# Split-ahead weight units: their loads wait for the activation or residual update that precedes them in the program

## The chip, the cores and the metric

The kernel runs on one core of one Trainium2 chip, as a single launch. The metric is the device time of that launch in microseconds (us), from the start of the program to its end. The times of the kernel before are three runs without a profiler, and one further execution that was profiled.

## The reference

A two-layer transformer over 512 tokens of width 1024, in float32. Each layer is a feed-forward block (FFN1), a mixer of several attention kinds, and a second feed-forward block (FFN2); every one adds to the residual stream x.

```python
def swiglu_ffn(x, g, w_gate, w_up, w_down):        # w_gate, w_up: 1024 x 2816; w_down: 2816 x 1024
    h = rmsnorm(x, g)
    return (jax.nn.silu(h @ w_gate) * (h @ w_up)) @ w_down

for i in range(DEPTH):                              # DEPTH = 2
    x = x + 0.5 * swiglu_ffn(x, ffn1_norm[i], ...)
    h = rmsnorm(x, mix_norm[i])
    if i % 2 == 0:
        x = x + even_mixer(h, cos, sin, ev_w_in[e], ..., ev_w_out[e])   # w_in 1024 x 2468, w_out 1024 x 1024
    else:
        x = x + odd_mixer(h, cos, sin, cos_i, sin_i, od_w_in[o], od_w_out[o])  # w_in 1024 x 2340
    x = x + 0.5 * swiglu_ffn(x, ffn2_norm[i], ...)
return rmsnorm(x, final_norm)
```

## The kernel before, in words

**Precision.** Every large product is made of three matmuls of a faster type. A float32 operand is split into a high part h (a rounded copy, by ScalarE, here ACT) and a low part l (the operand less h, by VectorE, here DVE). `mm3` then adds the products high-high, high-low and low-high. Activations are split once; weights are split as they arrive. `cut` (line 321) is the split of a weight tile: line 325 on ACT, line 326 on DVE.

**Weights of the feed-forward blocks.** `wunit` loads 128 x 1024 numbers into a buffer `raw` by SyncE's DMA queue (SP) and cuts them into `wh` and `wl`. There are four buffers of each.

**The feed-forward block.** `ffn` goes over eleven chunks of 256 hidden columns in three groups: chunks 0 to 3, 4 to 7 and 8 to 10. For each chunk `gate_up` makes the gate and up products and from them the activations `at`, split into two parts. From the second or third chunk on the up product is done by `seven`, a seven-product scheme (Strassen's kind): it loads two `raw` tiles (line 694), adds blocks of them on DVE (`s`, lines 720 to 723), splits the sums on ACT and DVE (lines 704 and 705), and combines the seven products (lines 737 to 751). A product on GpSimd (POOL) at line 777 multiplies the gate by the row scale `rb`. After each group `proj_T` does the down projection in four blocks of 256 output columns; each block ends with two residual updates `x[c] = ps * 0.5 + x[c]` on DVE (`update`, line 581). The gate and up products of a group read the normalised input of the block and not these updates.

**Split-ahead units.** The weights of the two mixers (60 units of at most 128 x 1024 numbers, 32 for the even layer and 28 for the odd one) are not cut in the mixers. The generator `cut_ahead` (line 267) does it earlier: it loads a unit into a buffer `craw` (two of them) by POOL's DMA queue, cuts it into `ch` and `cl` (two each), and stores both to scratch memory (`cuth`, `cutl`, line 282, also POOL's queue). The mixers later load the parts from there. One step of the generator cuts unit i, stores unit i-1 and issues the load of unit i+1.

**Where the program advances it.** `ffn` takes one step after the chunks 3, 5, 6 and 7, and weaves steps into the down projections: `per` units for each block of a down projection, and in the last group only in its first two blocks. The even-layer generator is advanced in FFN1 of layer 0 with `per` 3, the odd-layer one in FFN2 of layer 0 and then in FFN1 of layer 1 with `per` 2. What is left is run after the block.

**What sets the order.** The kernel is written on a layer that schedules at build time. It puts the instructions of each engine into a fixed queue, as its own model of time finds their operands and buffers ready, with the program's order as the priority, and adds the semaphores. An instruction may so be moved ahead of others that precede it in the program, if it doesn't depend on them. `pin` (keep in program order) prevents this, but only while `pinned[0]` is true, and that is set to false with the last slice of each block's first chunk. On the chip each engine runs its queue in order.

Of the kernel before, what the change touches and what calls it, by code (L numbers as in the profile page):

```python
# [13 lines left out]
F32 = mybir.dt.float32  # L14
# [51 lines left out]
def hybrid_kernel(tc, x_in, positions, ffn1_norm, ffn1_w_gate, ffn1_w_up, ffn1_w_down, mix_norm,  # L66
# [3 lines left out]
    nc = tc.nc  # L70
    with ExitStack() as ctx:
# [6 lines left out]
        def nm(p):  # L78
            cnt[0] += 1
            return f"{p}_{cnt[0]}"  # L80


        def ps_tile(tag):
            return psp.tile([P, S], F32, tag=tag, bufs=PSUM_BUFS[tag], name=nm("ps" + tag))

        def tile_(tag, dt=F32R):
            return sb.tile([P, S], dt, tag=tag, bufs=SB_BUFS[tag], name=nm(tag))
# [7 lines left out]
        def pin(ins):  # L95

            return tc.keep_in_program_order(ins) if pinned[0] else ins
# [29 lines left out]
        rows = cst.tile([16, P], F32, name="rows")  # L127
# [36 lines left out]
        x = [cst.tile([P, S], F32, name=f"x{c}") for c in range(NC)]  # L164
# [87 lines left out]


        cut_units = {}

        def wunit(src, a, b, rows=False, key=None, tag=("raw", "wh", "wl")):

            n = a * b  # L260
            if key in cut_units:
                res = []
                for part, t in zip(cut_units[key], tag[1:]):
                    w = sb.tile([P, 1024], F32R, tag=t, bufs=W_BUFS, name=nm(t))
                    nc.sync.dma_start(w[:, :n].bitcast(F32), part)
                    res.append(w[:, :n].rearrange("p (a b) -> p a b", a=a))
                return res
            h, l = cut(load_raw(src, a, b, rows, tag[0], RAW_BUFS), n, tag[1:], W_BUFS)
            return (h[:, :n].rearrange("p (a b) -> p a b", a=a), l[:, :n].rearrange("p (a b) -> p a b", a=a))

        def cut_ahead(units):

            raw = done = None

            def store():
                key, n, tiles = done
                parts = []
                for t, c in zip(tiles, "hl"):  # L280
                    d = scr.tile([P, n], F32, tag=nm("cut" + c), name=nm("cut" + c))
                    nc.gpsimd.dma_start(d, t[:, :n].bitcast(F32))
                    parts.append(d)
                cut_units[key] = parts

            for i, (key, src, a, b, rows) in enumerate(units):
                n = a * b
                if raw is None:
                    raw = load_raw(src, a, b, rows, "craw", 2, nc.gpsimd)
                now = key, n, cut(raw, n, ("ch", "cl"), 2)  # L290
                if done is not None:
                    store()
                done = now
                if i + 1 < len(units):
                    raw = load_raw(*units[i + 1][1:], "craw", 2, nc.gpsimd)
                yield
            store()

        def load_raw(src, a, b, rows, tag, bufs, queue=nc.sync):
            n = a * b  # L300
            raw = sb.tile([P, 1024], F32, tag=tag, bufs=bufs, name=nm(tag))
            r3 = raw[:, :n].rearrange("p (a b) -> p a b", a=a)
            if rows:
                o = 0
                for sap in src:
                    pin(queue.dma_start(r3[:, o:o + sap.shape[1]], sap))
                    o += sap.shape[1]
            elif isinstance(src, list):
                o = 0
                for sap, wd in src:  # L310
                    dst = r3[:, :, o:o + wd]
                    if len(sap.shape) == 4:
                        for c in range(a):
                            queue.dma_start(dst[:, c].rearrange("p (k d) -> p k d", k=sap.shape[2]), sap[:, c])
                    else:
                        queue.dma_start(dst, sap)
                    o += wd
            else:
                queue.dma_start(r3, src)
            return raw  # L320

        def cut(raw, n, tags, bufs):

            h, l = (sb.tile([P, 1024], F32R, tag=t, bufs=bufs, name=nm(t)) for t in tags)
            pin(nc.scalar.activation(h[:, :n], raw[:, :n], AF.Copy))  # L325
            pin(nc.vector.tensor_sub(l[:, :n], raw[:, :n], h[:, :n].bitcast(F32)))  # L326
            return h, l

        def mm3(ps, lh, ll, rh, rl, start, stop):
            nc.tensor.matmul(ps, lh, rh, start=start, stop=False)  # L330
            nc.tensor.matmul(ps, lh, rl, start=False, stop=False)  # L331
            nc.tensor.matmul(ps, ll, rh, start=False, stop=stop)  # L332
# [168 lines left out]
        def split(src, width=S, tag="f"):  # L501

            h, l = tile_(tag), tile_(tag)
            nc.scalar.copy(h[:, :width], src)
            nc.vector.tensor_sub(l[:, :width], src, h[:, :width].bitcast(F32))
            return h, l
# [70 lines left out]
        def update(c, ps, scale, nxt):  # L577
            if scale == 1.0:
                nc.vector.tensor_add(x[c], ps, x[c])
            else:  # L580
                nc.vector.scalar_tensor_tensor(x[c], ps, scale, x[c], op0=ALU.mult, op1=ALU.add)
            if nxt is not None:
                nxt.add(c)

# [168 lines left out]
        def gate_up(wg, wu, k, norm, sums, at):  # L753

            f0 = 256 * k
            if k < (1 if norm.source is None else 2):
                gate_up_pair(wg, wu, f0, norm, k == 0, sums.work, at)
                return
            psg = [ps_tile("T"), ps_tile("T")]
            for hf in range(2):  # L760
                h, l = wunit(wg[hf * 512:(hf + 1) * 512, f0:f0 + 256].rearrange("(c p) f -> p c f", p=P), 4, 256)
                if hf:
                    norm.rstd()
                for f in range(2):
                    if hf and f:
                        norm.finish()
                    for c in range(4):
                        xh, xl = norm.xg[hf * 4 + c]
                        mm3(psg[f], h[:, c, f * P:(f + 1) * P], l[:, c, f * P:(f + 1) * P], xh, xl,
                            hf == 0 and c == 0, hf == 1 and c == 3)  # L770
            rb = norm.rstd_row()
            gs, up = [], [tile_("p", F32) for _ in range(2)]
            for f in range(2):
                g = tile_("p", F32)
                nc.vector.tensor_mul(g, psg[f], rb)  # L775
                nc.scalar.activation(g, g, AF.Silu)  # L776
                nc.gpsimd.tensor_mul(g, g, rb)  # L777
                gs.append(g)
            seven(wu, f0, sums, up)
            nc.vector.tensor_mul(up[0], up[0], gs[0])  # L780
            at.append(split(up[0]))
            nc.vector.scalar_tensor_tensor(up[1], up[1], -1.0, gs[1], op0=ALU.mult, op1=ALU.mult)
            at.append(split(up[1]))

        def ffn(norm, wg, wu, wd, nxt, hook=None, ahead=iter(()), per=2, early=None):

            sums = Sums(norm)
            for p0, p1 in GROUPS:
                at = []
                for k in range(p0, p1):  # L790
                    gate_up(wg, wu, k, norm, sums, at)
                    if hook is not None and k < 6:
                        next(hook, None)
                    if k in (3, 5, 6, 7):
                        run(take(ahead, 1))
                for d0 in range(0, D, 256):
                    part = per / (4 * (p1 - p0)) if p1 < 11 or d0 < 512 else 0.0
                    run(weave(proj_T(wd[256 * p0:256 * p1], at, d0,
                                     lambda c, ps: update(c, ps, 0.5, nxt if p1 == 11 else None)), ahead, [part]))
                    if p1 == 11 and d0 == 0 and early is not None:  # L800
                        early()
# [741 lines left out]
        def hook():  # L1543
# [7 lines left out]
            tabs.extend(rope_tables(pos_f))  # L1551

        ev_ahead = cut_ahead(units_of(even_sources(), ev_w_out[0], "ev", EV_ORDERS))
        od_ahead = cut_ahead(units_of(odd_sources(), od_w_out[0], "od", OD_ORDERS))
        for layer in range(2):
            nm_ = Norm(1, layer)
# [46 lines left out]
```

## Time and profile before

| | us |
|---|---|
| median of 3 runs | 2079.99 |
| lowest and highest | 2079.59, 2083.52 |
| the profiled execution's own time | 2085.85 |
| its span, first to last instruction | 2084.1 |

Busy shares of the span: PE (TensorE matmuls) 95%, its weight loads 84%, DVE 67%, ACT 43%, POOL 21%. Mean DMA traffic 139 GB/s. The mean granted clock of TensorE is 0.978 of its full speed.

The profile has these views. The slices cut the span in 40 equal parts, 52.1 us each, and give busy tenths. The windows give sums for chosen stretches. The chain of waits follows the work that ended last back in time. The waits say who waited for whom. A tile's view says how often and when it was written or read.

### The profile page before, as it was taken

The numbers are of one execution on the slowest core, as the hardware profiler recorded it, in microseconds if no ns is written. First come the engines' busy times: TensorE is split into PE (matmuls) and PEld (weight loads), VectorE is DVE, ScalarE is ACT, GpSimd is POOL, SyncE is SP. The second block draws the span as 40 slices with busy tenths as digits, with TensorE's granted clock in tenths as the row PEclk, the third lists the DMA queues.
The fourth block names the chain that finished last, engine by engine and source line by source line (L and its number), as shares of the span: only waits on it lengthen the run. The fifth ranks groups of instructions, "written<-read, shape, count | busy, mean of one in ns | idle before, by whom it ended". The sixth has DMA issues, their size and how long they took to land.

```text
span 2084.1 us, 30295 instructions
## 1 busy us (share of the span) xinstructions
PE 1979.7 (95%) x11575; PEld 1751.5 (84%) x11575; DVE 1389.0 (67%) x2448; ACT 893.2 (43%) x1570; POOL 430.2 (21%) x584
## 2 busy tenths in 40 slices
PE   7897888899999999999999999999999999999998
PEld 5785776789997778889898888889998888889898
DVE  6775774754458768657477756747599778657464
ACT  6543442432456755324245323323326665324243
POOL 3544433301223411001010201101012211001012
PEclk9998899899999999999999999999999999999999
DMA  9797799673320123332323333323542223332321
GB/s 297 243 334 267 260 332 344 222 250 132 122 92 19 38 77 112 112 91 92 112 81 112 90 106 89 111 87 100 173 163 83 89 94 100 105 98 92 111 82 61
DMA packets 191811, 290.36 MB, mean 139 GB/s; under 512 B 12825, under 2 KB 154929, under 8 KB 191665
## 3 DMA queue, kind: packets, MB, share of 16 engines
q1 hardware_dynamic: 161152, 197.75, 29.6%
q0 software_dynamic: 23776, 84.30, 11.6%
q10 hardware_dynamic: 6736, 6.37, 0.9%
q8 instruction: 91, 1.49, 0.3%
q14 instruction: 56, 0.45, 0.1%
HBM read 230.11 MB, written 58.26 MB: 138 GB/s over the span
## 4 chain that ended last, share of the span: by engine, by line
PE 61%; issue 12%; DVE 12%; DMA 9%; POOL 3%; ACT 3%; DVEq 0%; POOLq 0%; ACTq 0%
PE psB L330 8%; PE psB L331 8%; PE psB L332 8%; PE psT L331 5%; PE psT L330 5%; PE psT L332 5%; PE psG L330 5%; PE psG L332 5%; PE psG L331 5%; DMA cutl<-cl 4%; DMA raw<-in_ffn_w_up_dram 2%; DMA craw<-in_ev_w_in_dram 2%; DVE cl L326 1%; ACT p L929 1%; DVE f L1428 1%
## 5 line engine op out<-in xcount | busy, mean ns | idle before, releaser
L326 DVE TENSOR_TENSOR wl<-raw,wh 128x1024 fp32r<-128x1024 f32 (+1 forms) x198 | 256.4, 1296 | 85.5 <-ACT wh L325 81.0
L777 POOL TENSOR_TENSOR p<-p,p 128x512 f32<-128x512 f32 x78 | 123.2, 1582 | 758.2 <-ACT p L776 730.4
L325 ACT ACTIVATE wh<-raw 128x1024 fp32r<-128x1024 f32 (+1 forms) x198 | 197.4, 1003 | 189.8 <-PE psB L331 162.1
L332 PE MATMUL psT<-xg,wl 128*128 128x512 f32 x704 | 275.6, 392 | 0.9 <-DVE wl L326 0.9
L330 PE MATMUL psT<-xg,wh 128*128 128x512 f32 x704 | 275.9, 392 | 0.0
L331 PE MATMUL psT<-xg,wh 128*128 128x512 f32 x704 | 275.1, 391 | 0.0
L330 PE MATMUL psB<-f,wh 128*128 128x512 f32 x656 | 255.5, 390 | 0.0
L331 PE MATMUL psB<-f,wh 128*128 128x512 f32 x656 | 255.3, 389 | 0.0
L332 PE MATMUL psB<-f,wl 128*128 128x512 f32 x656 | 255.2, 389 | 0.0
L330 PE MATMUL psG<-t7h,wh 128*128 128x256 f32 x624 | 185.1, 297 | 25.0 <-ACT k L737 22.1
L332 PE MATMUL psG<-t7h,wl 128*128 128x256 f32 x624 | 183.8, 294 | 6.7 <-DVE wl L705 6.7
L331 PE MATMUL psG<-t7l,wh 128*128 128x256 f32 x624 | 183.0, 293 | 0.0
L332 PEld LDWEIGHTS psT<-xg,wl 128*128 128x128 f32 x704 | 132.9, 189 | 29.3 <-DVE wl L326 1.3
L330 PEld LDWEIGHTS psT<-xg,wh 128*128 128x128 f32 x704 | 132.9, 189 | 26.7
L331 PEld LDWEIGHTS psT<-xg,wh 128*128 128x128 f32 x704 | 132.8, 189 | 26.5
L330 PEld LDWEIGHTS psG<-t7h,wh 128*128 128x128 f32 x624 | 127.1, 204 | 27.9 <-ACT k L737 23.6
L332 PE MATMUL psG<-xg,wl 128*128 128x256 f32 x468 | 135.1, 289 | 15.9 <-DVE wl L705 15.9
L330 PE MATMUL psB<-wh,xg 128*128 128x256 f32 x512 | 148.7, 290 | 0.4 <-DVE sa L927 0.4
L332 PE MATMUL psB<-wh,xg 128*128 128x256 f32 x512 | 145.3, 284 | 0.0
L331 PE MATMUL psB<-wl,xg 128*128 128x256 f32 x512 | 144.9, 283 | 0.0
L332 PEld LDWEIGHTS psB<-f,wl 128*128 128x128 f32 x656 | 123.1, 188 | 25.9
L776 ACT ACTIVATE p<-p 128x512 f32<-128x512 f32 x78 | 49.2, 631 | 222.1 <-DVE p L775 222.1
(312 smaller groups left out, 4802.2 us busy)
## 6 DMA issues: line engine op xcount, KB each, us to landing
raw<-in_ffn_w_down_dram SPq DMA_DIRECT2D x168, 256.0 KB, 3.3
raw<-in_ffn_w_gate_dram SPq DMA_DIRECT2D x80, 512.0 KB, 3.9
raw<-in_ffn_w_up_dram SPq DMA_DIRECT2D x80, 512.0 KB, 4.4
cuth<-ch POOLq DMA_DIRECT2D x44, 512.0 KB, 6.4
cutl<-cl POOLq DMA_DIRECT2D x44, 512.0 KB, 6.8
wl<-cutl SPq DMA_DIRECT2D x44, 512.0 KB, 3.7
wh<-cuth SPq DMA_DIRECT2D x44, 512.0 KB, 4.4
craw<-in_od_w_in_dram POOLq DMA_DIRECT2D x16, 512.0 KB, 6.6
```

The costliest lines, as they stand in the source:

```text
L325: pin(nc.scalar.activation(h[:, :n], raw[:, :n], AF.Copy))
L326: pin(nc.vector.tensor_sub(l[:, :n], raw[:, :n], h[:, :n].bitcast(F32)))
L330: nc.tensor.matmul(ps, lh, rh, start=start, stop=False)
L331: nc.tensor.matmul(ps, lh, rl, start=False, stop=False)
L332: nc.tensor.matmul(ps, ll, rh, start=False, stop=stop)
L776: nc.scalar.activation(g, g, AF.Silu)
L777: nc.gpsimd.tensor_mul(g, g, rb)
L929: nc.scalar.activation(pr[i], pr[i], AF.Exp, scale=-1.0, bias=ng[:, i:i + 1], accum_out=rs[:, i:i + 1])
L1428: nc.vector.match_replace(out=bd[i], in_to_replace=m8, in_values=bd[i], imm_value=-3e38)
```

## The change

The code gets a one-element list `mark`. `update` writes into it the first column of the residual tile it has just updated; `gate_up`, on its path with `seven`, the first column of the high part of the activation it has just split. With the new argument `gate=True`, which only `cut_ahead` passes, `load_raw` first copies that column on POOL into the first column of the new `craw` tile. The load overwrites it, and so comes after it. The value copied is never used.

```diff
+        mark = [None]
...
                 if raw is None:
-                    raw = load_raw(src, a, b, rows, "craw", 2, nc.gpsimd)
+                    raw = load_raw(src, a, b, rows, "craw", 2, nc.gpsimd, True)
...
                 if i + 1 < len(units):
-                    raw = load_raw(*units[i + 1][1:], "craw", 2, nc.gpsimd)
+                    raw = load_raw(*units[i + 1][1:], "craw", 2, nc.gpsimd, True)
...
-        def load_raw(src, a, b, rows, tag, bufs, queue=nc.sync):
+        def load_raw(src, a, b, rows, tag, bufs, queue=nc.sync, gate=False):
             n = a * b
             raw = sb.tile([P, 1024], F32, tag=tag, bufs=bufs, name=nm(tag))
+            if gate:
+
+                nc.gpsimd.tensor_copy(raw[:, 0:1], mark[0])
...
                 nc.vector.scalar_tensor_tensor(x[c], ps, scale, x[c], op0=ALU.mult, op1=ALU.add)
+            mark[0] = x[c][:, 0:1]
...
             at.append(split(up[1]))
+            mark[0] = at[-1][0][:, 0:1].bitcast(F32)
```

## Rows read from the trace of the kernel before

**Rows 1.** The page's 40 slices: busy tenths, granted clock, DMA share.
```profile
PE   7897888899999999999999999999999999999998
...
PEclk9998899899999999999999999999999999999999
DMA  9797799673320123332323333323542223332321
```

**Rows 2.** Chain of waits in order of time: start us, us, what.
```profile
15.90 0.80 PE psS L330
```

**Rows 3.** Windows of FFN1, layer 0: us, engines' busy us (instructions), clock, DMA share, GB/s.
```profile
0.00:124.00 124.00, 104.19 (x523) 87.63 (x524) 93.24 (x128) 73.12 (x99) 58.11 (x98) 0.97 0.87 283
124.00:181.00 57.00, 52.32 (x235) 42.92 (x234) 29.87 (x54) 15.69 (x18) 20.47 (x32) 1.00 0.91 302
181.00:300.00 119.00, 91.35 (x491) 82.11 (x492) 88.29 (x111) 51.53 (x71) 53.26 (x76) 0.83 0.82 279
300.00:348.00 48.00, 48.00 (x214) 39.74 (x213) 24.25 (x28) 15.75 (x16) 16.02 (x26) 1.00 0.97 346
348.00:431.00 83.00, 63.89 (x367) 58.01 (x366) 56.55 (x75) 31.75 (x43) 25.91 (x33) 0.86 0.62 227
431.00:461.00 30.00, 30.00 (x136) 24.79 (x135) 17.09 (x24) 11.21 (x18) 0.64 (x1) 1.00 0.91 302
```

**Rows 4.** Windows of FFN2, layer 0, the same six stages (PE, PEld, DVE, ACT, POOL).
```profile
777.00:865.00 88.00, 85.64 (x495) 75.56 (x494) 70.53 (x105) 43.79 (x62) 14.22 (x9) 0.98 0.34 102
865.00:908.00 43.00, 43.00 (x191) 35.62 (x190) 19.38 (x24) 8.52 (x9) 0.00 (x0) 1.00 0.37 110
908.00:995.00 87.00, 87.00 (x543) 78.88 (x543) 63.61 (x89) 35.23 (x49) 13.22 (x8) 1.00 0.30 92
995.00:1036.00 41.00, 41.00 (x183) 33.95 (x182) 17.15 (x21) 7.55 (x8) 0.00 (x0) 1.00 0.37 115
1036.00:1102.00 66.00, 66.00 (x411) 59.81 (x410) 47.37 (x67) 25.60 (x37) 9.58 (x6) 1.00 0.28 84
1102.00:1131.00 29.00, 29.00 (x129) 24.01 (x129) 17.72 (x26) 13.47 (x20) 0.00 (x0) 1.00 0.33 102
```

**Rows 5.** The tile craw: ns min/median/max, first and last start us.
```profile
L325 ACT ACTIVATE ch<-craw x60: 630/1057/1067, 13.9 to 395.1; 128x1024 fp32r<-128x1024 f32 x44, 128x512 fp32r<-128x512 f32 x8, 128x840 fp32r<-128x840 f32 x4, 128x584 fp32r<-128x584 f32 x4
...
L316 POOL DMA_DIRECT2D craw<-in_od_w_in_dram x20: 717/766/811, 225.4 to 331.9; - x20
...
DMA to landing us min/median/max: 3.0/6.1/9.1
```

**Rows 6.** Windows of FFN1, layer 0, of ACT's instructions on ch alone.
```profile
0.00:124.00 124.00, 15.28 (x15) 0.97 0.87 283
124.00:181.00 57.00, 8.05 (x8) 1.00 0.91 302
181.00:300.00 119.00, 18.80 (x22) 0.83 0.82 279
300.00:348.00 48.00, 8.50 (x8) 1.00 0.97 346
348.00:431.00 83.00, 7.37 (x7) 0.86 0.62 227
```

**Rows 7.** PE's waits, 777 to 1131 us: total, times, longest us; the longest.
```profile
PE psX L560 <- DVE p L546: 2.0, 1, 2.0
```

**Rows 8.** Waits of all engines, 0 to 461 us: total, times, longest us.
```profile
DVE cl L326 <- DMA cutl<-cl: 44.5, 13, 6.9
...
ACT ch L325 <- DMA craw<-in_od_w_in_dram: 36.4, 12, 6.6
...
PE psG L332 <- DVE wl L705: 22.6, 9, 6.7
```

**Rows 9.** POOL's groups by shape: busy us, mean ns; idle before.
```profile
L843 POOL TENSOR_TENSOR sm<-sm,keep 128x1 f32<-128x1 f32 x4 | 2.2, 546 | 0.3
...
L842 POOL TENSOR_SCALAR sm<-sm,sm 128x1 f32<-128x1 f32 x4 | 1.1, 265 | 6.1 <-ACT pt L832 6.1
```

## The prediction

> **What bounds the kernel now.** I read the page's slices first [rows 1]: TensorE (PE) is 90% busy or more almost everywhere after the first fifth of the span, while in the first eight slices (0 to 417 us) it stands at 70 to 90%, its granted clock dips to 80 and 90%, and the 16 DMA engines are 60 to 90% busy, against mostly 10 to 40% after the first quarter. So the one stretch with slack is the first feed-forward block (FFN1 of layer 0, 0 to 461 us); the others run at PE's pace.
>
> How much slack: I cut this block into its six stages (gate/up of chunks 0 to 3, down of group 0, gate/up 4 to 7, down, gate/up 8 to 10, down) and set each beside the same stage of FFN2 of layer 0 (777 to 1131 us), which does the same matmuls with the ordinary traffic [rows 3, 4]. PE works across stage borders, so I count matmuls: the excess of a stage is its length less its matmuls at the later block's pace.
> - A, 0 to 124: 124 - 523 x 88/495 = 31 us, of which 16 are the start: the chain of waits reaches the first weight matmul at 15.90 us [rows 2].
> - B, 124 to 181: 57 - 235 x 43/191 = 4.
> - C, 181 to 300: 119 - 491 x 87/543 = 40.
> - D, 300 to 348: 48 - 214 x 41/183 = 0.
> - E, 348 to 431: 83 - 367 x 66/411 = 24.
> - F, 431 to 461: 30 - 136 x 29/129 = -1.
>
> Without the start that is 15 + 4 + 40 + 0 + 24 - 1 = 82 us, the most that a change confined to this block's side work can give back. In C and E the granted clock is 0.83 and 0.86, that is, part of the time at 1.2 instead of 2.4 GHz; in the later block's same stages it is 1.00, and one PE wait of 2.0 us is the longest there [rows 4, 7].
>
> What makes the excess: the split-ahead units. All 60 are cut between 13.9 and 395.1 us, and the loads from od_w_in, whose generator is first advanced in FFN2, start at 225.4 us [rows 5]. The order in each engine's queue is made at build time; nothing that these loads read depends on the program's progress, so they went as far forward as buffers allowed. Counted by stage [rows 6]: 15, 8, 22, 8, 7 and none. Per unit that is 1.0 us in A, 0.5 in B, 1.83 in C, 0.0 in D, 3.4 in E. The way it costs is in the waits [rows 8]: ACT stands at `ch` for a landing load, DVE stands at `cl` until an earlier store of `cutl` has landed, the weight splits queued behind them come late, and PE waits for `wl`. Down stages hide it (weights are split several units ahead), the seven-product stages don't.
>
> **The change part by part.**
> *60 copies of one column on POOL.* The trace before has no such copy; the nearest rows are POOL instructions on 128x1, 265 and 546 ns [rows 9]. At most 60 x 0.55 = 33 us on an engine that is 21% busy; at the low end nothing is seen of it. A gain is excluded, as it only adds work. I take nothing, since it precedes a load of 6.1 us median landing [rows 5] that is not on PE's path by itself. Loads and stores keep their number and their bytes.
>
> *What the copy waits for.* For the 28 odd-layer units this moves the work: the first load cannot start before the split of chunk 3 in FFN2 of layer 0 (about 865 us). For the 32 even-layer units: the first waits for the split of chunk 3 (124 us now), so A is free of units: 15 us gained, and B starts earlier by that.
> By the code the 32 go: 1 after chunk 3, 12 in the first down, 3 after chunks 5 to 7, 12 in the second down, 4 in the third. A down stage has carried 8 (B and D, DMA share 0.91 and 0.97 [rows 3]), so I let 8 run in B, the 5 left over with 3 of their own in C, 8 in D, 4 in E, 4 in F. At the stages' own price per unit: B 4 as before; C 8 x 1.83 = 15 instead of 40, a gain of 25; D 0; E 4 x 3.4 = 14 instead of 24, a gain of 10; F 4 x 0.5 = 2 instead of nothing. Sum 15 + 25 + 10 - 2 = 48 us gained.
>
> *What the odd-layer units cost where they land.* 24 in FFN2 of layer 0 (1, 8, 3, 8, 4), 4 in FFN1 of layer 1 (1, 3): 23 in down stages, 5 in gate/up. The cover now is a DMA share of 0.28 to 0.37 and a PE that waits for nothing [rows 4, 7]. Downs: between 0 (D) and 0.5 us (B) a unit, 0 to 12 us; I take 6, midway, as a down with 8 units is exactly what both rows are. Gate/up: between 0 (A to F differ from the later block only by these units, and a lone unit may vanish in that slack) and 3.4 (E); I take C's 1.83, since most of the cases counted are there: 5 x 1.83 = 9. Together 15 us lost.
>
> *What is queued behind the wait.* On POOL the unit's own load issues, the stores of the units, and the gate products `p` of L777 and L641. A copy that waits for a residual update holds them until the end of one block of a down projection, 43/4 = 10.8 us at the longest [rows 4]. The gate products of a group come in the program after the last update of the group before, so I cost this at nothing; if a copy is placed ahead of a product that is ready, PE's next splits come late, which the rate of E covers. SP's queue gets no instruction; its weight loads meet less traffic up to 124 us and in C.
>
> **Sum.** 48 - 15 = 33 us. Against the profiled execution's own 2085.85 us (span 2084.1 and 1.75 around it) that is 2053; the median of the runs shown, 2079.99, is 5.9 us lower, and by it the time is 2047 us. Ends: if every unit that stays in or comes to a seven-product stage costs E's 3.4 us and downs 0.5, the gain is 15 + (40 - 27) + 10 - 2 - (17 + 12) = 7 us, 2073; if none costs anything at the lower density, 82 us, 1998.
>
> **The rivals.**
> 1. *Full relief.* Price is a matter of saturation, not of units: C's 22 units kept the DMA share at 0.82 and the clock at 0.83, while 8 units would not. Then E's, C's and A's excess all go and the later blocks swallow 28 units in traffic that is a third of the DMA engines: -65 to -85 us, about 2005. For it: D, with 8 units and no excess. Against: E, which has only 7 units, a DMA share of 0.62, and the dearest price per unit.
> 2. *Slower: the late start shows in the later blocks.* A gated load starts at an update instead of as soon as a buffer is free; its cut keeps a fixed place in ACT's and DVE's order, so ACT stands there for up to the 6.1 us landing, and the splits behind it reach PE late, in blocks where PE now waits for nothing. At E's price for all 28: 95 us lost against 48 gained, +47, 2127. It decides from 48/28 = 1.7 us per odd-layer unit, which is close to C's 1.83. For it: C and E. Against: 23 of the 28 come in down stages, at 0 to 0.5.
> The Trainium skill, page "DMA: Bandwidth & Descriptors", section "Rules for kernel authors", says to issue a transfer early, compute, and wait for its semaphore late. By that rule this change is wrong in direction and this rival would be the outcome. The trace so far bears it out only in part: in FFN1 the early loads made their own cuts, and the weights behind them, late.
> 3. *Moved, not removed.* The even-layer units alone, 32 units squeezed into 124 to 461 us, keep those stages as saturated as now: only A's 15 us and part of C are gained and most is paid back later: -5 to -14, about 2070.
> 4. *It does not act.* If the copies' sources were written before the loads could start anyway, nothing moves: 2080. That holds for some even-layer units, not for the odd ones, which run at 225 us before any of FFN2 exists.
>
> **How the numbers follow.** Forecast, 2015 to 2066: 0.59. Rival 1: 0.14. Rival 2: 0.13. Rival 3: 0.09. Rival 4: 0.05. A measurement of this kernel tells about 0.2% (4 us) from no change; faster is the forecast with rivals 1 and 3, 0.82, the same 0.05, slower 0.13. The range takes in rival 3 and most of rival 1: 2003 to 2080; the forecast's own is 2015 to 2066.
>
> **What would show it.** The `ch` cuts: none before about 109 us, 32 in FFN1 of layer 0, 24 in FFN2, 4 in FFN1 of layer 1. FFN1 of layer 0 ends near 413 instead of 461 us, its granted clock near 0.95 or more; the first split of chunk 3 comes at about 109. FFN2 of layer 0 takes 354 + 12 us with a DMA share near 0.55. Wrong would be: cuts still packed in the first 400 us; PE waits for `wl` of several us per chunk in FFN2; POOL's `p` products waiting on the copies; or mixers that wait for their stored weights.

## The result, and the profile after

The changed kernel takes 2093.41 us (median of 4 runs, 2090.83 to 2097.14) against 2080.18 for the kernel before beside it: ratio 1.0062, 95% interval 1.0042 to 1.0081. It is slower by about 13 us, or 0.6%. Forecast were 2047 us and faster; the measured time lies outside the range of 2003 to 2080.

The profiled execution (2097.14 us, span 2095.3) shows where. I cut the span at the end of the last residual update of each block, read from DVE's timeline:

| block, us | before | after | change | forecast |
|---|---|---|---|---|
| FFN1, layer 0 | 461.9 | 431.1 | -30.8 | -48 |
| even mixer | 314.8 | 317.5 | +2.7 | 0 |
| FFN2, layer 0 | 355.3 | 392.7 | +37.4 | +12 |
| FFN1, layer 1 | 353.4 | 355.3 | +1.9 | +3 |
| all that follows | 598.7 | 598.7 | 0.0 | 0 |

So the work went where it was forecast to go, and what it gave back in the first block it lost, and more, in the third. The slices of the page, as in [rows 1]:

```profile
PE   8996897999989999979889999999999999999998
...
PEclk9998898999999999999989999999999999999999
DMA  5377576473310133845834254323542233332321
```

The first two slices are a little fuller (8 and 9 tenths against 7 and 8) at a lower DMA share. A new dent stands in slices 18, 20 and 21 (7, 8 and 8 tenths where there were 9), and slices 17 and 20 show a DMA share of 80% where it was 30%. The tile `craw` says which units are there (columns as in [rows 5]):

```profile
L329 ACT ACTIVATE ch<-craw x60: 613/1059/1065, 116.6 to 1266.3; 128x1024 fp32r<-128x1024 f32 x44, 128x512 fp32r<-128x512 f32 x8, 128x840 fp32r<-128x840 f32 x4, 128x584 fp32r<-128x584 f32 x4
...
L305 POOL COPY craw<-x x39: 174/577/1712, 133.8 to 1257.9; 128x1 f32<-128x1 f32 x39
L318 POOL DMA_DIRECT2D craw<-in_ev_w_in_dram x24: 747/755/819, 143.3 to 276.6; - x24
L305 POOL COPY craw<-f x21: 179/653/1677, 105.9 to 1230.8; 128x1 f32<-128x1 f32 x21
L320 POOL DMA_DIRECT2D craw<-in_od_w_in_dram x20: 717/766/818, 840.3 to 1028.7; - x20
```

The odd-layer loads moved from 225 to 840 us: 23 of the 28 cuts are in FFN2 of layer 0, 5 in FFN1 of layer 1. FFN1 of layer 0 by its six stages, to be set beside [rows 3], and FFN2 as a whole, first before the change and then after it:

```profile
0.00:109.00 109.00, 101.98 (x528) 86.35 (x529) 79.44 (x120) 59.73 (x85) 21.73 (x41) 1.00 0.42 130
109.00:163.00 54.00, 51.31 (x231) 42.09 (x229) 26.56 (x48) 15.40 (x18) 24.98 (x41) 1.00 0.83 275
163.00:264.00 101.00, 74.84 (x430) 66.98 (x430) 65.29 (x83) 37.69 (x50) 37.33 (x47) 0.86 0.61 206
264.00:329.00 65.00, 61.19 (x290) 51.20 (x290) 36.18 (x45) 21.19 (x25) 31.48 (x50) 1.00 0.82 276
329.00:385.00 56.00, 45.80 (x264) 40.92 (x265) 40.47 (x54) 22.68 (x32) 13.59 (x16) 0.88 0.44 148
385.00:431.00 46.00, 42.89 (x223) 36.52 (x223) 28.52 (x43) 17.77 (x29) 9.15 (x14) 0.99 0.72 233
```
```profile
776.60:1131.90 355.30, 352.94 (x1949) 308.89 (x1949) 237.06 (x331) 135.13 (x185) 37.02 (x23) 1.00 0.32 98
```
```profile
749.00:1141.00 392.00, 362.43 (x1947) 315.19 (x1946) 263.70 (x352) 156.97 (x206) 98.21 (x119) 0.96 0.52 174
```

The first window ends at 109 us because that is where the forecast put the end of stage A; the last split of chunk 3 ends at 105.8 us (123.1 before) on ACT's timeline, and no cut runs before 116.6. Stages C and E run at a clock of 0.86 and 0.88, little above the 0.83 and 0.86 before the change. FFN2 has the same matmuls as before in 37 us more, at a clock of 0.96: PE stands still for 29.6 us of its window against 2.4, and its busy time is 9.5 us longer. Its waits name the mechanism (total, times, longest; 749 to 1141 us):

```profile
ACT ch L329 <- DMA craw<-in_od_w_in_dram: 84.5, 17, 12.1
...
DVE cl L330 <- ACT ch L329: 53.5, 15, 9.6
```
```profile
PE psG L336 <- DVE wl L710: 10.4, 4, 7.3
PE psG L334 <- ACT wh L709: 9.9, 2, 8.1
```

ACT waits 84.5 us for loads from od_w_in, 17 times (101 us with those from od_w_out), where nothing of the kind stood in FFN2 before. How one such wait reaches PE is seen in ACT's and PE's own timelines at the end of the first down projection (start, length, line; in brackets the idle time before and what ended it):

```profile
886.75 1.06 ACT L329 ACTIVATE ch<-craw 128x1024 fp32r<-128x1024 f32 x1 [11.55 <-DMA craw<-in_od_w_in_dram]
887.71 0.61 ACT L709 ACTIVATE wh<-raw 128x512 fp32r<-128x512 f32 x1
888.23 1.05 ACT L329 ACTIVATE ch<-craw 128x1024 fp32r<-128x1024 f32 x1
889.18 1.05 ACT L709 ACTIVATE wh<-raw 128x1024 fp32r<-128x1024 f32 x1
900.65 1.06 ACT L329 ACTIVATE ch<-craw 128x1024 fp32r<-128x1024 f32 x1 [10.42 <-DMA craw<-in_od_w_in_dram]
901.62 1.04 ACT L709 ACTIVATE wh<-s 128x1024 fp32r<-128x1024 f32 x1
```
```profile
902.71 0.58 PE L334 MATMUL psG<-xg,wh 128*128 128x256 f32 x1 [8.06 <-ACT wh L709]
```

The weight split of chunk 4 (`wh` of L709, of a sum `s` that DVE had ready at 880.0 us) stands behind a `ch` that waits 10.42 us for its load; PE waits 8.06 us for that split. The load itself was late because its copy waited for an update: the chain of waits goes round, update, copy, load, cut (start, length, what):

```profile
878.35 1.83 POOL craw L305 x2
880.36 6.28 DMA craw<-in_od_w_in_dram
886.75 1.07 ACT ch L329
...
892.07 1.11 POOL craw L305
893.47 7.11 DMA craw<-in_od_w_in_dram
900.65 1.07 ACT ch L329
```

There is a second path. At the end of the second down projection (1041.2 us) ACT stands 12.13 us at a cut, the weight splits behind it come late, and so does the `raw` buffer that they free. SP waits 13.9 us for this and issues the next weight load only at 1042.40 us. DVE stands for that load at L725, and behind it stands the `wl` that PE needs:

```profile
1027.97 8.52 DMA craw<-in_od_w_in_dram
...
1036.59 1.07 ACT ch L329
...
1041.24 1.14 DVE wl L710
1042.40 8.23 DMA raw<-in_ffn_w_up_dram
...
1051.34 1.22 DVE wl L710
```
```profile
1052.61 0.58 PE L336 MATMUL psG<-xg,wl 128*128 128x256 f32 x1 [7.25 <-DVE wl L710]
```

PE's waits of 0.6 us or more in FFN2 sum to 28 us on its timeline. Of these 23 stand within 20 us of the ends of the first two down projections (892.0 and 1041.2 us), in the first seven-product chunk of the next group.

### The profile page after: what moved, and what is told of

Its sections match the earlier page's. It is cut to its first block, busy times and chain, and to the rows that moved or that the text cites. A ratio compares the mean times of both kernels' runs of the same rounds, so it can differ in the third digit from the quotient of the medians.

```text
span 2095.3 us, 30564 instructions
## 1 busy us (share of the span) xinstructions
PE 1978.7 (94%) x11575; PEld 1746.7 (83%) x11575; DVE 1393.1 (66%) x2448; ACT 902.2 (43%) x1570; POOL 473.7 (23%) x644
## 4 chain that ended last, share of the span: by engine, by line
PE 59%; DVE 12%; issue 11%; DMA 8%; POOL 5%; ACT 4%; ACTq 0%; SPq 0%; POOLq 0%; DVEq 0%
PE psB L334 7%; PE psB L335 7%; PE psB L336 7%; PE psT L335 6%; PE psT L334 6%; PE psT L336 6%; PE psG L334 5%; PE psG L335 4%; PE psG L336 4%; DMA craw<-in_od_w_in_dram 2%; DMA cutl<-cl 2%; DMA craw<-in_ev_w_in_dram 2%; PE psC L966 1%; DVE f L1434 1%; ACT p L935 1%
## 5 line engine op out<-in xcount | busy, mean ns | idle before, releaser
L330 DVE TENSOR_TENSOR wl<-raw,wh 128x1024 fp32r<-128x1024 f32 (+1 forms) x198 | 260.7, 1319 | 69.4 <-ACT wh L329 68.6
L782 POOL TENSOR_TENSOR p<-p,p 128x512 f32<-128x512 f32 x78 | 131.7, 1690 | 612.2 <-ACT p L781 578.9
L330 DVE TENSOR_TENSOR cl<-craw,ch 128x1024 fp32r<-128x1024 f32 (+3 forms) x60 | 67.8, 1132 | 136.6 <-ACT ch L329 105.5
L329 ACT ACTIVATE ch<-craw 128x1024 fp32r<-128x1024 f32 (+3 forms) x60 | 58.0, 967 | 230.9 <-DMA craw<-in_od_w_in_dram 84.5
L334 PE MATMUL psG<-xg,wh 128*128 128x256 f32 x468 | 136.1, 291 | 20.1 <-ACT wh L709 20.1
L334 PEld LDWEIGHTS psG<-t7h,wh 128*128 128x128 f32 x624 | 123.1, 197 | 33.2 <-ACT k L742 23.3
```

## The experiments

All runs against the kernel before on the same chip. Block lengths are cut as above; "wait" is the idle time of ACT just before the cuts `ch` in FFN2 of layer 0, summed from its timeline. FFN2 without units takes 355.3 us. Block lengths come from one profiled execution each. Without units they repeat well (355.3 twice for FFN2, 353.4 to 353.5 for FFN1 of layer 1). With units they scatter: the five runs that have the changed kernel's source for FFN1 of layer 0 (after, e7, e8, e9, e13) took 422.9 to 431.1 us there, so differences of a few us are not firm.

| run | ratio (95%) | FFN1, layer 0 | mixer | FFN2 (units) | wait | FFN1, layer 1 |
|---|---|---|---|---|---|---|
| before | 1 | 461.9 | 314.8 | 355.3 (0) | 0 | 353.4 |
| after | 1.0062 (1.0042, 1.0081) | 431.1 | 317.5 | 392.7 (23) | 101 | 355.3 |
| e1_split_only | 0.9993 (0.9981, 1.0006) | 426.0 | 316.6 | 381.6 (23) | 78 | 353.2 |
| e3_odd_only | 0.9975 (0.9961, 0.999) | 416.1 | 315.0 | 391.0 (23) | 99 | 353.3 |
| e4_even_only | 1.014 (1.0121, 1.0159) | 440.6 | 358.9 | 355.3 (0) | 0 | 353.4 |
| e5_odd_start | 0.9979 (0.9964, 0.9993) | 415.9 | 313.9 | 396.4 (28) | 74 | 353.5 |
| e6_odd_per1 | 0.9995 (0.998, 1.0009) | 414.7 | 314.3 | 378.0 (15) | 96 | 375.2 |
| e7_per1 | 1.0068 (1.0044, 1.0093) | 422.9 | 317.7 | 380.1 (15) | 96 | 375.7 |
| e8_no_store | one run | 429.1 | 318.9 | 378.6 (23) | 89 | - |
| e9_no_cut | one run | 429.8 | 314.4 | 362.1 (no cuts) | 0 | - |
| e13_no_load | one run | 430.3 | 317.3 | 356.8 (23) | 38 | - |
| e12_gate_pin | 0.9937 (0.9915, 0.9959) | 412.9 | 314.2 | 389.4 (22) | 71 | 353.3 |
| e10_pin_all | 0.99 (0.9885, 0.9915) | 415.5 | 314.6 | 375.9 (22) | 60 | 353.4 |
| e11_pin_odd | 0.9896 (0.9879, 0.9912) | 412.9 | 313.3 | 373.8 (22) | 61 | 353.7 |
| e14_pin_odd_per1 | 0.9814 (0.9801, 0.9828) | 411.5 | 314.1 | 354.7 (14) | 24 | 354.5 |
| e15_gate_pin_per1 | 0.9891 (0.9876, 0.9905) | 419.6 | 314.3 | 366.2 (14) | 50 | 360.4 |

**e1: the update's mark alone is undone.**

```diff
-            mark[0] = x[c][:, 0:1]
```

> The copies wait for the last activation split only, no longer for residual updates. Theory 1 (a loop: update, copy, load, cut on ACT, weight splits queued behind the cut, matmuls, next update): without the update in it the loop is gone. FFN2 of layer 0, 355 us before and 393 after the change, falls to 360 to 370; FFN1 of layer 0 stays at 425 to 435 (462 before); time 2055 to 2072 us. Theory 2 (the 24 odd-layer units cost their traffic and their cuts in FFN2 whatever starts them): FFN2 stays at 385 to 395, time 2088 to 2096.

FFN2 took 381.6 us, between the two ranges: the wait for updates is worth about 11 of the 37 us, and the rest stays without it.

**e3 and e4: the two generators apart.** `cut_ahead` gets an argument and passes it on in place of `True`.

```diff
-        ev_ahead = cut_ahead(units_of(even_sources(), ev_w_out[0], "ev", EV_ORDERS))
+        ev_ahead = cut_ahead(units_of(even_sources(), ev_w_out[0], "ev", EV_ORDERS), False)   # e3; e4: od_ahead
```

> Only the odd-layer units are held by copies; the even-layer ones are loaded as before the change. Both theories: FFN2 of layer 0 as after the change, about 390 us. Even units run in the first 215 us as before, none after it, so FFN1 is 415 to 430; if holding the even units back is worth something by itself it is over 440. Time 2075 to 2090 us.

> Only the even-layer units are held; the odd-layer ones are free to run far ahead, as before the change. Both theories: FFN2 of layer 0 back at 355 us, FFN1 at 455 to 480, since it carries all 60 units and has the loop of updates and loads for the 32 even ones as well. Time 2078 to 2100 us.

Holding back the odd-layer units alone frees 46 us of FFN1 (462 to 416), and holding the even-layer ones as well gives 15 of these back (431; 8 in the pair e6 and e7). In e4 the odd-layer cuts queue behind the held even ones in the two `craw` buffers and run from about 412 to 613 us, 23 of them in the even mixer, which takes 44 us more; this I had not foreseen, and FFN1's 440.6 us lie below the range. The price of odd-layer units is similar in the three blocks: 46 us for 28 of them in FFN1, 44 for the 23 in the mixer, 39 for the 28 after the change, 1.4 to 1.9 us a unit.

**e5: one mark for all odd-layer units, no wait for updates.**

```diff
             raw = done = None
+            first = [mark[0]] if gate else None
...
-                nc.gpsimd.tensor_copy(raw[:, 0:1], mark[0])
+                nc.gpsimd.tensor_copy(raw[:, 0:1], gate[0])
```

> Even-layer units free as before the change; every odd-layer unit waits for one and the same thing, the split of chunk 3 in FFN2 of layer 0, so that 28 units stay out of FFN1 but none waits for an update. Theory 1: FFN2 360 to 370 us, FFN1 415 to 430, time 2045 to 2060. Theory 2: FFN2 385 to 395, time 2073 to 2085.

FFN2 took 396.4 us, 1 us above the range of theory 2, with no copy that waits for an update. My theory of the loop fell with this as the main cause.

**e6 and e7: one odd-layer unit for each block instead of two.**

```diff
-                ffn(n2, ffn2_w_gate[layer], ffn2_w_up[layer], ffn2_w_down[layer], n1, None, od_ahead)
+                ffn(n2, ffn2_w_gate[layer], ffn2_w_up[layer], ffn2_w_down[layer], n1, None, od_ahead, 1)   # and FFN1, layer 1
```

> As the run that holds only the odd-layer units, with one of them for each block of a down projection instead of two, so 14 fall to FFN2 of layer 0 and 14 to FFN1 of layer 1. Theory 3 (the price comes from density: units that spill past the end of a down projection into the next chunk's seven products): FFN2 358 to 367 us instead of 391, FFN1 of layer 1 354 to 362 instead of 353, time 2045 to 2058 us. Theory 4 (a unit costs about 1.4 us wherever it runs): FFN2 373 to 378, FFN1 of layer 1 370 to 375, time 2073 to 2080.

> The changed kernel with one odd-layer unit for each block of a down projection instead of two. Theory 3: FFN2 358 to 367 us instead of 393, FFN1 of layer 1 354 to 362, time 2060 to 2072. Theory 4: both at 370 to 378, time 2088 to 2096.

Density by itself is not it: half the units cost 22 to 25 us in each of two blocks, 1.5 to 1.7 us a unit, as theory 4 has it. Each cut now waited longer: 96 us in all for 15 of them (for 27 of these the profile names no releaser).

**e8, e9 and e13: a unit's parts taken away.** In e8 the odd-layer `store` returns at once; in e9 the tile is stored as it is; in e13 one tile is loaded and then cut again for each unit.

```diff
-                now = key, n, cut(raw, n, ("ch", "cl"), 2)
+                now = key, n, (cut(raw, n, ("ch", "cl"), 2) if keep else (raw, raw))   # e9
...
+                if not keep and i + 1 < len(units):                                    # e13
+                    nc.gpsimd.tensor_copy(raw[:, 0:1], mark[0])
+                elif i + 1 < len(units):
```

> The changed kernel with the odd-layer units loaded and cut ahead but not stored, and the odd mixer cutting its own weights; only FFN2 of layer 0 is to be compared. A unit's traffic there falls from 1.5 to 0.5 MB at most. If traffic is what costs: FFN2 364 to 374 us (393 with the change). If it is the cuts that stand in ACT's and DVE's queues for their loads: 383 to 395.

> The changed kernel with the odd-layer units loaded and stored twice but not cut, and the odd mixer cutting its own weights; only FFN2 of layer 0 is to be compared. Traffic is kept, ACT and DVE have nothing of the units in their queues. If the waiting cuts are what costs: FFN2 355 to 364 us. If traffic: 378 to 393.

> The changed kernel in which the odd-layer generator loads one tile and then cuts and stores that same tile 28 times, each time behind the copy that waits; the odd mixer cuts its own weights. Only FFN2 of layer 0 is to be compared. The cuts' work and the stores stay, the wait for a load is gone. Theory W: 356 to 368 us. Theory B: 382 to 395.

These three, of one run each, bound the cause. Cuts, stores and waiting copies together, without the loads, cost 1.5 us (e13); loads and stores without the cuts cost 7 (e9); the 37 us need both, a cut and a load that it waits for. Taking away the stores, two thirds of the traffic (e8), is worth 14 us, less than the range for traffic and more than the one for cuts. e13's window, and ACT's wait at `ch`, now for a copy:

```profile
748.00:1104.00 356.00, 352.67 (x1947) 308.34 (x1946) 265.52 (x352) 159.62 (x206) 74.86 (x93) 1.00 0.50 167
```
```profile
ACT ch L334 <- POOL craw L299: 26.7, 18, 6.4
```

Engine work in e13 is that of the changed kernel (DVE 265.5 us, ACT 159.6) at a clock of 1.00, and e9 runs at a higher DMA share than the changed kernel (0.57 against 0.52): neither work nor traffic alone is what PE lost.

**e10 to e12: the cuts kept in program order.** The order of the queues is made at build time; kept in order, a cut cannot be put ahead of what the program names before it.

```diff
-            pin(nc.scalar.activation(h[:, :n], raw[:, :n], AF.Copy))
+            pin_ = tc.keep_in_program_order if hold else pin
+            pin_(nc.scalar.activation(h[:, :n], raw[:, :n], AF.Copy))      # and the subtraction on DVE
```

> The kernel before, without any copy; the cuts of the odd-layer units alone are kept in the program's order on ACT and DVE, so that they come in FFN2 of layer 0 and FFN1 of layer 1, and their loads go out as soon as a buffer is free, a whole step ahead of the cut. Theory W (the price is ACT and DVE standing at the cut of a load that has not landed): FFN2 of layer 0 356 to 366 us, FFN1 of layer 0 415 to 420, time 2040 to 2054. Theory B (the price is the cuts' own 2.3 us of work ahead of the weight splits): FFN2 382 to 395, time 2070 to 2080.

> As the run that keeps the odd-layer cuts in program order, with the even-layer cuts kept so too: 12 of them fall into each of the first two down projections of FFN1, three for each block of about 10.8 us, with a load of about 6 us each. Theory W: FFN2 356 to 366 us, FFN1 of layer 0 425 to 455 since loads three to a block cannot keep up, time 2052 to 2085. Theory B: FFN2 382 to 395, time over 2085.

> The changed kernel (copies that wait) with all cuts kept in program order as well. The load starts at an update and its cut stands half a block, about 5.4 us, behind in ACT's order. Theory W: the waits stay, about as long as the load less 5.4 us, FFN2 of layer 0 368 to 388 us against 393, time 2075 to 2093. Theory B: FFN2 388 to 396, time 2088 to 2100.

Without the copies, kept order alone (e11, e10) cuts the price in FFN2 by half, to 18 and 21 us, between the ranges of the two theories: at two units to a block ACT still waits about 60 us at the cuts. With the copies (e12) it takes 3 us off FFN2. Its 389.4 us lie in the range of theory B, which e13 excludes, and its 2068.18 us lie below both ranges. In FFN1 of layer 0 e10 took 415.5 us where I had expected 425 to 455; with the even-layer cuts free (e11) it took 412.9. With the copies, the kept order of the even-layer cuts helped FFN1 by 18 us (431.1 to 412.9), but by 3 in the pair with one unit to a block (422.9 in e7, 419.6 in e15).

The sum of ACT's waits does not give the price: 96 us of waiting cost 23 us in e6, 74 us cost 41 in e5, and 71 us cost 34 in e12.

**e14 and e15: kept order and one unit to a block.** e14 is e11 and e15 is e12, with the edit of e6.

> No copies; odd-layer cuts kept in program order, one to a block of a down projection (10.8 us) instead of two. If the waits of ACT at the cuts are the whole price, a load of about 6.5 us that goes out a full block ahead has landed, and FFN2 of layer 0 takes 356 to 364 us (374 with two to a block), FFN1 of layer 1 353 to 360, time 2040 to 2052. If what is left of the price is the cuts' place at the border to the next group, whatever they wait for, FFN2 is 368 to 376, FFN1 of layer 1 364 to 372, time 2058 to 2070.

> The changed kernel, copies that wait for updates kept, with all cuts kept in program order and one odd-layer unit to a block. The load starts at an update and its cut stands about a block behind in ACT's order. If the price is ACT standing at the cut, and not the copies' waiting, FFN2 of layer 0 is 356 to 366 us (393 with the change, 387 with kept order alone), FFN1 of layer 1 353 to 362, time 2045 to 2058. If waiting for the update itself costs, FFN2 stays over 375, time over 2068.

In e14 the price is gone: 354.7 and 354.5 us for blocks that take 355.3 and 353.4 without units. Windows of FFN2 and FFN1 of layer 1, and ACT's waits in FFN2:

```profile
726.00:1080.00 354.00, 350.94 (x1947) 307.21 (x1946) 252.63 (x343) 149.00 (x197) 65.19 (x65) 1.00 0.49 155
1080.00:1435.00 355.00, 353.97 (x1963) 310.06 (x1962) 252.08 (x338) 148.13 (x196) 70.44 (x71) 1.00 0.50 160
```
```profile
ACT wh L710 <- PE psT L336: 37.7, 16, 4.4
...
ACT ch L330 <- DMA craw<-in_od_w_in_dram: 21.1, 5, 5.8
ACT wh L710 <- PE psB L336: 18.3, 4, 4.8
```

ACT again waits mostly for PE to free buffers, which means that it is ahead; 21 us at the cuts do no harm. At 2041.49 us, ratio 0.9814, this kernel is faster than the kernel before and than the changed one.

What differs between e11 and e14 is seen at the end of the first down projection, 859.9 us in e11 and 856.3 in e14. First e11, then e14:

```profile
860.98 1.06 ACT L330 ACTIVATE ch<-craw 128x1024 fp32r<-128x1024 f32 x1 [9.70 <-DMA craw<-in_od_w_in_dram]
```
```profile
840.44 1.06 ACT L330 ACTIVATE ch<-craw 128x1024 fp32r<-128x1024 f32 x1 [5.80 <-DMA craw<-in_od_w_in_dram]
...
849.95 0.63 ACT L710 ACTIVATE wh<-raw 128x512 fp32r<-128x512 f32 x1 [4.38 <-PE psB L336]
855.34 1.06 ACT L710 ACTIVATE wh<-raw 128x1024 fp32r<-128x1024 f32 x1 [4.76 <-PE psB L336]
```

In e11 a cut waits 9.70 us right at that end, with the splits of the next group behind it, and PE stands 6.14 us until 879.05, among the first products of the next group. The same comes once more after the second down projection (8.81 us), and these are PE's only waits over 2 us in FFN2. In e14 the last cut before that end is 16 us ahead of it, and the splits behind it wait for PE. Its load was not early: POOL issued it at 835.5 us, 5 us ahead of the cut, and ACT waited 5.80 us. By POOL's and ACT's timelines six of e14's 14 loads for FFN2 go out 4.5 to 6.9 us ahead of their cuts and eight go out 18 us or more ahead; in the changed kernel all 23 go out 4.7 to 9.0 us ahead.

e15, which differs by the copies (and by the even-layer cuts in kept order), pays 11 and 7 us, and ACT waits 50 us at its cuts in FFN2 against 24. (The 387 us in its expectation are e12's 389.4.)

## Why the prediction was wrong

**What held.** The slack stood in FFN1 of layer 0 and the odd-layer units were half of it: 46 of the 82 us came back when they alone were held (e3). Stage A was read nearly right: the split of chunk 3 was forecast at about 109 us and came at 105.8. The units landed as counted, 32, 23 (24 forecast) and 5 (4). The copies' own time does not show: e13 has one before each cut in FFN2 and loses 1.5 us.

**The step that failed** is "what the odd-layer units cost where they land": 15 us forecast, 39.3 measured (37.4 and 1.9). It took the down stages' price of 0 to 0.5 us a unit from B and D [rows 3, 6]. But the price of a unit that makes ACT wait in a down stage is paid in the next stage: after the change PE lost 8.06 us among the first products of chunk 4 for cuts queued in the down before. The trace before shows the same at the border of D and E (349 us):

```profile
345.22 1.06 ACT L325 ACTIVATE ch<-craw 128x1024 fp32r<-128x1024 f32 x1 [4.95 <-DMA craw<-in_od_w_out_dram]
...
353.17 1.06 ACT L325 ACTIVATE ch<-craw 128x1024 fp32r<-128x1024 f32 x1 [5.94 <-DMA craw<-in_od_w_out_dram]
354.14 1.04 ACT L704 ACTIVATE wh<-s 128x1024 fp32r<-128x1024 f32 x1
```
```profile
355.23 0.58 PE L330 MATMUL psG<-xg,wh 128*128 128x256 f32 x1 [3.33 <-ACT wh L704]
```

So waits that begin in D were paid in E, and D looked free; how much of C's and E's excess comes from the downs before them was not taken apart. Assigning the excess to the stage in which PE stood still gave prices that could not be moved with the units. One price for all, 82 us over 60 units or 1.4 us, would have said +39 for 28 units. That this is the measured number to the microsecond is luck: the same units cost 44 us for 23 in the mixer (e4) and next to nothing in e14, so no one price holds.

**The second term** mis-sized was FFN1: 31 us gained and not 48. By the prediction's own count C's excess is 101 - 430 x 87/543 = 32 us with 8 cuts, where 15 were forecast from 1.83 us a unit; E's is 56 - 264 x 66/411 = 14, as forecast. The count is rough: over all six stages it gives 40 us gained where the block gained 31. Holding the even-layer units is itself a loss against letting them go, 15 us by e3 against the changed kernel and 8 by e6 against e7, though A gained its 15. The mixer's 2.7 us had no term.

**The rivals.** Rival 2 had the mechanism and the place: ACT at a cut whose load has not landed, the splits behind it late, in FFN2. Its price was 3.4 us a unit and came to 1.4; its point of decision, 1.7 us, came down to (30.8 - 2.7)/28 = 1.0 with the smaller gain, and so it decided. Its reason was only partly right: the start at an update is worth 11 us (e1), and loads held by nothing but buffers (e5) cost as much. What costs is a cut in ACT's queue ahead of splits that PE needs soon, while its load, of 6.3 and 7.1 us in the chain shown, has not landed. Two things can prevent this, a load that goes out well ahead of its cut and a cut that stands away from the first splits of the next group. e14 has some of both, and no run separates them; the three waits of 4.4 to 5.8 us inside its first down projection cost PE nothing, which speaks for the place.

The Trainium skill's page "DMA: Bandwidth & Descriptors", section "Rules for kernel authors", has the rule that spoke against the change: issue the transfer early, compute, wait for its semaphore late. The runs agree with it as far as they go: FFN2 takes 392.7 us where every odd-layer load goes out at most 9.0 us ahead of its cut, and 354.7 in e14, where eight of 14 go out 18 us or more ahead, though the other six do not.

**What stays open.** Why the build-time order puts a cut where its load has not landed is inferred from the order, not measured. Whether distance or place did more in e14 stays open too. The 7 us of e9, the 14 of e8, the copies' 11 and 7 us in e15, and the roughly 40 us that the even-layer units still cost in FFN1 (411.5 us in e14, against 355.3 and a start of 16) were not taken apart.

## What to carry to other kernels

A side job's price belongs to the queue in which its instruction waits, and the engine that starves may show it one stage later; so before a price read from one stage is moved elsewhere, look in the queue for the instruction that waited. Delaying a load relieves the place it leaves, but if the instruction that consumes it keeps its place in the queue, everything queued behind stands until the load has landed. Here such a wait cost PE most where the next products needed fresh splits, after a down projection, and nothing where splits were ready. Holding the consumers in program order and spacing them, with no hold on the loads, removed the price (e14); holding the loads added to it.

## What the runs showed of the hardware that was not expected

A POOL copy of one column, 128x1, took 577 ns at the median and 174 to 1712 ns, more than the 265 and 546 ns of the POOL rows on the same shape [rows 9]. And TensorE kept its granted clock at 1.00 through FFN2 with the DMA engines at a share of 0.49 to 0.50 and 23 and 14 cuts in the queues (e13, e14): the 0.96 after the change stands in the run where PE waits.
